# A two-layer attention, linear-attention and MLP backbone on one core: the MLP phases' arithmetic leaves GpSimd for VectorE

## The chip, the cores and the metric

The kernel runs on one core of a Trainium2 chip. The metric is device time of one execution in microseconds. Three executions of the kernel before took 2741.91, 2745.80 and 2748.45 us; the median is 2745.8 us. Engines are named as in the profile: PE multiplies matrices, DVE is VectorE, ACT is ScalarE, POOL is GpSimd, SP issues the DMAs.

## The reference

512 latent tokens and 256 context tokens of width 1024 pass through two layers. Each layer mixes tokens (windowed attention and a gated linear attention, merged and projected) and then runs a squared-ReLU MLP of width 4096. Cut to what the change touches:

```
def rms_norm(x, g):
    y = x * rsqrt(mean(x * x) + EPS); return y * g
def modulate(h, shift, scale):
    return h * (1.0 + scale) + shift
def squared_relu_mlp(h, w1, w2):
    return square(relu(h @ w1)) @ w2
# per layer, after the token mixing:
x  = x  + gt2  * squared_relu_mlp(modulate(rms_norm(x,  g_norm2), sh2,  sc2),  w_ff1, w_ff2)
xc = xc + gt2c * squared_relu_mlp(modulate(rms_norm(xc, g_norm2), sh2c, sc2c), w_ff1, w_ff2)   # not in the last layer
```

All of it is in float32; the last layer has no context stream in its MLP, so its token width is 512 where the first layer's is 768.

## The kernel before, in words

**Split products.** A float32 operand is split in two: a high part, rounded to the matmul's reduced float32 format by ACT (`act(hi, src, Copy)`), and a low part, source minus high part, by a `tensor_tensor` subtraction on DVE or POOL. `split` does it for activations and `unit` for a 512 KB weight tile (names `raw`, `whi`, `wlo`). A product is three matmuls: high by high, high by low, low by high.

**The MLP** (`mlp`) runs over 8 chunks of 512 hidden columns. Chunk 0 multiplies `w_ff1` directly (`ff1`, `relu2`). After its products `seven_tokens` builds the token factors of a 2 by 2 block scheme with seven products instead of eight: for each of 4 row blocks four sums `b` (high plus low part of the normed input H), then differences that are split into `T` and back into H. Chunks 1 to 7 use `seven_weights` (weight factors `s1` to `s4`, each split) and `seven` (seven products into three PSUM banks, with `cw`, `cz` and `c` holding partial results, and `ended` squaring the ReLU and splitting it into `hid`). Every chunk ends with the second product: four panels of `w_ff2`, each added into x by a DVE instruction on line 1065.

**The junction.** The last thing before chunk 0's second product is the norm of tokens 256 to 511 (`late`), whose result H the first product, the token factors and so all later chunks need. Below, "junction" means this stretch: 1060 to 1105 us in the first layer, 2378 to 2421 us in the second. "Chunk loop" means chunks 1 to 7: about 1130 to 1590 us and 2440 to 2710 us.

**Norm.** `norm` makes 8 row blocks of H. Blocks 1, 3 and 5 go through `split` with the low part on POOL, the others through line 337 on DVE.

**What sets the order.** Instructions of an engine run in order. That order is chosen when the program is built, by a scheduler that steps a timing model and picks among the instructions that are ready; tile pools decide when a buffer is free: 3 `raw`, 4 `whi`, 4 `wlo`, 8 `c` or `b` tiles, 5 `mm` banks in the MLP. The same helper lines stand for all users: line 97 is every ACT copy or activation, line 100 every subtraction, line 106 every addition, line 103 every multiplication; so the tile names tell them apart.

Of the kernel before, what the change touches and what calls it, by code (L numbers as in the profile page):

```python
# [10 lines left out]
F32 = mybir.dt.float32  # L11
# [19 lines left out]
CH = 512  # L31
# [28 lines left out]
class Net:  # L60
# [259 lines left out]
    def norm(self, x, t0, n, which, H, rs=None):  # L320

        nc = self.nc
        tt = slice(t0, t0 + n)
        c = int(t0 >= SEQ)
        A, sh = self.A[which], self.mod[:, 0 if which == 1 else 3]
        rs = self.scales(x, t0, n) if rs is None else rs
        for k in range(KD):
            xr = self.t2([128, n], "xr")
            b = sh[:, k, c:c + 1]
            nc.vector.scalar_tensor_tensor(out=xr, in0=x[:, k, tt], scalar=A[:, k, c:c + 1], in1=rs, op0=ALU.mult, op1=ALU.mult)  # L330
            if k % 2 and k < 7:
                nc.vector.tensor_scalar_add(xr, xr, b)
                self.split(H, xr, (slice(None), k, tt), nc.gpsimd)
            else:
                hi = H.hi[:, k, tt]
                self.act(hi, xr, ACTF.Identity, bias=b)
                nc.vector.scalar_tensor_tensor(out=H.lo[:, k, tt], in0=xr, scalar=b, in1=hi.bitcast(F32),
                                               op0=ALU.add, op1=ALU.subtract)
# [585 lines left out]
    def seven_weights(self, w, c0):  # L924

        nc = self.nc
        raws = []
        for r in (0, 512):
            raw = self.wp.tile([128, 4, 2, 128], F32, name="raw", tag="raw", bufs=3)
            nc.sync.dma_start(out=raw, in_=w[r:r + 512, c0:c0 + 256].rearrange("(k p) (f c) -> p k f c", p=128, f=2))  # L930
            raws.append(raw)
        a11, a21 = raws[0][:, :, 0], raws[0][:, :, 1]
        a12, a22 = raws[1][:, :, 0], raws[1][:, :, 1]
        s1, s2, s3, s4 = [self.t2([128, 4, 128], n) for n in ("s1", "s2", "s3", "s4")]
        self.add(s1, a21, a22)
        self.sub(s2, s1, a11)
        self.sub(s3, a11, a21, nc.gpsimd)
        self.sub(s4, a12, s2)
        out = {}
        for group in ((("a11", a11), ("s2", s2)), (("s1", s1), ("a12", a12)), (("s3", s3), ("s4", s4)), (("a22", a22),)):  # L940
            hi = self.wp.tile([128, 2, 4, 128], F32R, name="whi", tag="whi")
            lo = self.wp.tile([128, 2, 4, 128], F32R, name="wlo", tag="wlo")
            for i, (name, src) in enumerate(group):
                self.act(hi[:, i], src, ACTF.Copy)
                self.sub(lo[:, i], src, hi[:, i].bitcast(F32))
                out[name] = [Pair(hi[:, i, k], lo[:, i, k]) for k in range(4)]
        return out

    def seven_tokens(self, pool, H, n):

        nc = self.nc
        wide = self.wide([128, 2, 2, 4, n], F32R, "T12")
        t4 = pool.tile([128, 2, 4, n], F32R, name="T4", bufs=1)
        T = {"t1": Pair(wide[:, 0, 0], wide[:, 0, 1]), "t2": Pair(wide[:, 1, 0], wide[:, 1, 1]),
             "t4": Pair(t4[:, 0], t4[:, 1])}
        at = {"b11": (0, 0), "b21": (4, 0), "b22": (4, n), "t3": (0, n)}

        def temp(name):
            return pool.tile([128, n], F32, name=name, tag="c", bufs=8)

        for k in range(4):
            b = {}
            for name, (r, t0) in (("b12", (0, n)), ("b11", (0, 0)), ("b22", (4, n)), ("b21", (4, 0))):
                b[name] = temp(name)
                self.add(b[name], H.hi[:, r + k, t0:t0 + n].bitcast(F32), H.lo[:, r + k, t0:t0 + n].bitcast(F32), nc.gpsimd)
            self.sub(b["b11"], b["b12"], b["b11"])
            self.split(T["t1"], b["b11"], (slice(None), k))
            self.sub(b["b11"], b["b22"], b["b11"])
            self.split(T["t2"], b["b11"], (slice(None), k))
            self.sub(b["b21"], b["b21"], b["b11"])  # L970
            self.split(T["t4"], b["b21"], (slice(None), k))
            self.sub(b["b22"], b["b22"], b["b12"])
            self.split(H, b["b22"], (slice(None), k, slice(n, 2 * n)))
        out = {name: [Pair(t.hi[:, k], t.lo[:, k]) for k in range(4)] for name, t in T.items()}
        for name, (r, t0) in at.items():
            out[name] = [Pair(H.hi[:, r + k, t0:t0 + n], H.lo[:, r + k, t0:t0 + n]) for k in range(4)]
        return out

    def seven(self, pool, W, X, n, hid):

        nc = self.nc

        def part(ps, a, b, start):
            self.product(ps, n, list(zip(W[a], X[b])), start)

        def temp(name):
            return pool.tile([128, n], F32, name=name, tag="c", bufs=8)

        def ended(c, f, t0):
            h = hid[f]  # L990
            nc.vector.scalar_tensor_tensor(out=c, in0=c, scalar=0.0, in1=c, op0=ALU.max, op1=ALU.mult)
            self.split(h, c, (slice(None), slice(t0, t0 + n)), nc.gpsimd)

        a, b, c = [self.bank("mm") for _ in range(3)]
        s, w, z, c11, c12, c21, c22 = [temp(name) for name in ("cs", "cw", "cz", "c11", "c12", "c21", "c22")]
        part(a, "a11", "b11", True)
        self.act(s, a[:, :n], ACTF.Copy)
        part(b, "s2", "t2", True)
        self.add(w, b[:, :n], s)
        part(c, "s1", "t1", True)  # L1000
        self.add(z, c[:, :n], s)
        part(a, "a12", "b21", False)
        self.act(c11, a[:, :n], ACTF.Relu)
        ended(c11, 0, 0)
        part(b, "s3", "t3", False)
        self.add(c22, b[:, :n], z)
        ended(c22, 1, n)
        part(c, "s4", "b22", False)
        self.add(c12, c[:, :n], w)
        ended(c12, 0, n)  # L1010
        part(b, "a22", "t4", False)
        self.add(c21, b[:, :n], s)
        ended(c21, 1, 0)

    def mlp(self, l, x, H, groups, late, before_last, done):


        nc, io, tc = self.nc, self.io, self.tc
# [4 lines left out]
        with tc.tile_pool(name="ml", bufs=1, reuse_waits="tile") as pool:  # L1023
            for ch in range(nch):
# [10 lines left out]
                if ch == 0:  # L1035
                    us = [self.panel(io["w_ff1"][l], p * 256) for p in range(2)]
# [15 lines left out]
                    before_last()  # L1052
                for part in (groups if ch == nch - 1 else [whole]):
                    for p in range(4):
                        us = self.panel(io["w_ff2"][l], p * 256, rows=(ch * CH, (ch + 1) * CH), lo_eng=nc.gpsimd)
                        for f in range(2):
                            j = p * 2 + f
                            for t0, n in part:
                                c, xx = int(t0 >= SEQ), x[:, j, t0:t0 + n]
                                ps = self.mm()  # L1060
                                self.product(ps, n, [(Pair(us[0].hi[:, k, f * 128:(f + 1) * 128],
                                                           us[0].lo[:, k, f * 128:(f + 1) * 128]),
                                                      Pair(h.hi[:, t0:t0 + n], h.lo[:, t0:t0 + n]))
                                                     for k, h in enumerate(hid)])
                                nc.vector.scalar_tensor_tensor(out=xx, in0=ps[:, :n],  # L1065
                                                               scalar=self.mod2[:, 5, j, c:c + 1], in1=xx,
                                                               op0=ALU.mult, op1=ALU.add)
                            self.tick(0.7)
                    if ch == nch - 1:
                        done(part)  # L1070
# [136 lines left out]
```

## Time and profile before

| | |
|---|---|
| median of three executions | 2745.8 us |
| the profiled execution's own time | 2742.91 us |
| its span in the profile | 2741.1 us |
| granted PE clock, mean | 0.972 |
| PE busy | 2579.2 us (94%) |
| DVE busy | 1634.7 us (60%) |
| ACT busy | 1151.7 us (42%) |
| POOL busy | 780.1 us (28%) |

An engine's busy time does not tell whether it holds up another; that is read from the idle time ahead of an instruction and from what ended it (in brackets in a timeline). A duration of a DVE or POOL instruction runs from its start to its end, so time in which it is held is inside it. The granted clock is a share of PE's full 2.4 GHz; 0.5 is 1.2 GHz.

### The profile page before, as it was taken

To read this page: it belongs to the slowest core of one execution; us is meant where nothing else is said; L and a number is where in the kernel's file an instruction comes from. 1 tells how busy PE (TensorE), PEld (TensorE's weight loads), DVE (VectorE), ACT (ScalarE), POOL (GpSimd) and SP (SyncE) were. 2 spreads that over 40 slices of the span, in tenths; PEclk is the share of its full clock that TensorE was granted. 3 is DMA by queue.
4 is the path that set the end of the run, shared out by engine and by line. 5 is a ranking of instruction groups with operands and counts; after the bars stand their busy time and mean duration, and the time that the engine had idled before them with its cause. 6 is when DMAs were issued, how large, how long until landed. Compare 5 with 4: busy or idle time off the path is not lost. (4 is left out here: it accounts for less than half of the span.)

```text
span 2741.1 us, 43359 instructions
## 1 busy us (share of the span) xinstructions
PE 2579.2 (94%) x17227; PEld 2267.8 (83%) x17227; DVE 1634.7 (60%) x3127; ACT 1151.7 (42%) x2526; POOL 780.1 (28%) x574
## 2 busy tenths in 40 slices
PE   6899999999999898999999988999999998889999
PEld 3888887878878787888888988888888887879898
DVE  4566777534454468644455565787654446677765
ACT  3556554435252334322222245655445334434343
POOL 1413221211120214232223354233122112253444
PEclk7999999999999999999999999999999999999999
DMA  7212123233343433243333241222222225322333
GB/s 252 68 36 72 45 49 100 89 101 93 100 139 90 159 109 93 85 131 107 124 116 123 77 149 47 66 63 68 88 77 85 62 85 177 108 92 90 103 106 111
DMA packets 223838, 269.82 MB, mean 98 GB/s; under 512 B 18480, under 2 KB 185684, under 8 KB 223508
## 3 DMA queue, kind: packets, MB, share of 16 engines
q1 hardware_dynamic: 223636, 267.05, 32.0%
q8 instruction: 135, 2.21, 0.3%
q14 instruction: 67, 0.55, 0.1%
HBM read 244.21 MB, written 22.81 MB: 97 GB/s over the span
## 5 line engine op out<-in xcount | busy, mean ns | idle before, releaser
L97 ACT ACTIVATE whi<-raw 128x1024 fp32r<-128x1024 f32 (+1 forms) x350 | 333.0, 953 | 585.7 <-DMA raw<-in_w_ff 167.2
L920 PE MATMUL mm<-hid,whi 128*128 128x512 f32 (+1 forms) x1664 | 427.3, 347 | 21.0 <-ACT hid L97 10.1
L100 POOL TENSOR_TENSOR wlo<-raw,whi 128x1024 fp32r<-128x1024 f32 x126 | 306.1, 2434 | 321.4 <-ACT whi L97 295.4
L920 PEld LDWEIGHTS mm<-hid,whi 128*128 128x128 f32 x1664 | 290.5, 192 | 72.5 <-issue 11.9
L100 DVE TENSOR_TENSOR wlo<-raw,whi 128x1024 fp32r<-128x1024 f32 (+1 forms) x224 | 238.2, 1064 | 141.2 <-ACT whi L97 137.6
L920 PE MATMUL mm<-hid,wlo 128*128 128x256 f32 (+1 forms) x832 | 281.5, 343 | 0.0
L173 PE MATMUL mm<-H,whi 128*128 128x512 f32 (+1 forms) x760 | 263.0, 347 | 4.8 <-POOL H L100 4.3
L172 PE MATMUL mm<-H,whi 128*128 128x512 f32 (+1 forms) x760 | 264.0, 350 | 2.9 <-ACT H L97 2.1
L174 PE MATMUL mm<-H,wlo 128*128 128x512 f32 (+1 forms) x760 | 261.7, 345 | 0.0
L1065 DVE SCALAR_TENSOR_TENSOR x<-mm,mod,x 128x512 f32<-128x512 f32 (+1 forms) x208 | 126.6, 622 | 125.4 <-PE mm L920 125.1
L920 PE MATMUL mm<-H,whi 128*128 128x384 f32 (+1 forms) x896 | 197.6, 311 | 0.0
L100 POOL TENSOR_TENSOR hid<-c,hid 128x384 fp32r<-128x384 f32 (+1 forms) x112 | 112.4, 1013 | 248.3 <-ACT hid L97 244.0
L920 PEld LDWEIGHTS mm<-hid,wlo 128*128 128x128 f32 x832 | 158.8, 191 | 18.1
L173 PEld LDWEIGHTS mm<-H,whi 128*128 128x128 f32 x760 | 146.6, 193 | 21.0 <-POOL H L100 4.8
L172 PEld LDWEIGHTS mm<-H,whi 128*128 128x128 f32 x760 | 146.4, 194 | 19.9 <-ACT H L97 2.8
L174 PEld LDWEIGHTS mm<-H,wlo 128*128 128x128 f32 x760 | 146.5, 193 | 16.3 <-issue 0.2
L920 PEld LDWEIGHTS mm<-H,whi 128*128 128x128 f32 x896 | 149.8, 190 | 9.4 <-issue 4.9
L920 PE MATMUL mm<-T,whi 128*128 128x384 f32 (+1 forms) x672 | 145.2, 309 | 0.0
L920 PE MATMUL mm<-H,wlo 128*128 128x384 f32 (+1 forms) x448 | 137.5, 309 | 1.1 <-DVE wlo L100 1.1
L97 ACT ACTIVATE p<-p,nm 128x512 f32<-128x512 f32 (+1 forms) x128 | 98.1, 768 | 71.6 <-DVE nm L456 71.6
L453 DVE CUSTOM_DVE_ANT_0 p<-S,mask 128x512 f32<-128x512 f32 (+1 forms) x128 | 96.3, 752 | 46.3 <-PE S L451 44.5
L100 POOL TENSOR_TENSOR mz<-mz,az 128x256 f32<-128x256 f32 (+1 forms) x32 | 36.4, 1137 | 301.3 <-ACT az L97 189.5
(276 smaller groups left out, 6768.3 us busy)
## 6 DMA issues: line engine op xcount, KB each, us to landing
raw<-in_w_ff SPq DMA_DIRECT2D x136, 512.0 KB
raw<-in_w_mod SPq DMA_DIRECT2D x96, 512.0 KB
raw<-in_w_in SPq DMA_DIRECT2D x88, 512.0 KB
raw<-in_w_branch_attn SPq DMA_DIRECT2D x64, 256.0 KB
raw<-in_w_out SPq DMA_DIRECT2D x32, 512.0 KB
raw<-in_w_in SPq DMA_DIRECT2D x32, 256.0 KB
ya<-yd SPq DMA_DIRECT2D x32, 256.0 KB
raw<-in_w_branch_gla SPq DMA_DIRECT2D x16, 512.0 KB
```

The costliest lines, as they stand in the source:

```text
L97: return self.nc.scalar.activation(out=out, in_=in_, func=func, **kw)
L100: (eng or self.nc.vector).tensor_tensor(out=out, in0=a, in1=b, op=ALU.subtract)
L172: nc.tensor.matmul(ps[:, :n], lhsT=wh, rhs=xh, start=(i == 0), stop=False)
L173: nc.tensor.matmul(ps[:, :n], lhsT=wh, rhs=xl, start=False, stop=False)
L174: nc.tensor.matmul(ps[:, :n], lhsT=wl, rhs=xh, start=False, stop=(i == len(ks) - 1))
L453: nc.vector.tensor_tensor_reduce(out=p[:, :nk], in0=S[:, s0:s0 + nk], in1=mask, scale=1.0, scalar=-3e38, op0=ALU.add, op1=ALU.max, accum_o ...
L920: self.nc.tensor.matmul(ps[:, :n], lhsT=a, rhs=b, start=start and i == j == 0, stop=i == last and j == 2, skip_group_check=not start)
L1065: nc.vector.scalar_tensor_tensor(out=xx, in0=ps[:, :n], scalar=self.mod2[:, 5, j, c:c + 1], in1=xx, op0=ALU.mult, op1=ALU.add)
```

## The change

Five places lose their POOL argument, so that the same instruction is issued on DVE: the low parts of norm's blocks 1, 3 and 5 (norm runs in the token mixing's start too), the weight factor `s3`, the sums `b` of `seven_tokens`, the low parts of `hid` in `ended`, and the low parts of the `w_ff2` panels. In the MLP phases POOL has no arithmetic left; in the token mixing it keeps its own.

```
--- before.py
+++ after.py
@@ -330,7 +330,7 @@
             nc.vector.scalar_tensor_tensor(out=xr, in0=x[:, k, tt], scalar=A[:, k, c:c + 1], in1=rs, op0=ALU.mult, op1=ALU.mult)
             if k % 2 and k < 7:
                 nc.vector.tensor_scalar_add(xr, xr, b)
-                self.split(H, xr, (slice(None), k, tt), nc.gpsimd)
+                self.split(H, xr, (slice(None), k, tt))
             else:
                 hi = H.hi[:, k, tt]
                 self.act(hi, xr, ACTF.Identity, bias=b)
@@ -934,7 +934,7 @@
         s1, s2, s3, s4 = [self.t2([128, 4, 128], n) for n in ("s1", "s2", "s3", "s4")]
         self.add(s1, a21, a22)
         self.sub(s2, s1, a11)
-        self.sub(s3, a11, a21, nc.gpsimd)
+        self.sub(s3, a11, a21)
         self.sub(s4, a12, s2)
         out = {}
         for group in ((("a11", a11), ("s2", s2)), (("s1", s1), ("a12", a12)), (("s3", s3), ("s4", s4)), (("a22", a22),)):
@@ -962,7 +962,7 @@
             b = {}
             for name, (r, t0) in (("b12", (0, n)), ("b11", (0, 0)), ("b22", (4, n)), ("b21", (4, 0))):
                 b[name] = temp(name)
-                self.add(b[name], H.hi[:, r + k, t0:t0 + n].bitcast(F32), H.lo[:, r + k, t0:t0 + n].bitcast(F32), nc.gpsimd)
+                self.add(b[name], H.hi[:, r + k, t0:t0 + n].bitcast(F32), H.lo[:, r + k, t0:t0 + n].bitcast(F32))
             self.sub(b["b11"], b["b12"], b["b11"])
             self.split(T["t1"], b["b11"], (slice(None), k))
             self.sub(b["b11"], b["b22"], b["b11"])
@@ -989,7 +989,7 @@
         def ended(c, f, t0):
             h = hid[f]
             nc.vector.scalar_tensor_tensor(out=c, in0=c, scalar=0.0, in1=c, op0=ALU.max, op1=ALU.mult)
-            self.split(h, c, (slice(None), slice(t0, t0 + n)), nc.gpsimd)
+            self.split(h, c, (slice(None), slice(t0, t0 + n)))
 
         a, b, c = [self.bank("mm") for _ in range(3)]
         s, w, z, c11, c12, c21, c22 = [temp(name) for name in ("cs", "cw", "cz", "c11", "c12", "c21", "c22")]
@@ -1052,7 +1052,7 @@
                     before_last()
                 for part in (groups if ch == nch - 1 else [whole]):
                     for p in range(4):
-                        us = self.panel(io["w_ff2"][l], p * 256, rows=(ch * CH, (ch + 1) * CH), lo_eng=nc.gpsimd)
+                        us = self.panel(io["w_ff2"][l], p * 256, rows=(ch * CH, (ch + 1) * CH))
                         for f in range(2):
                             j = p * 2 + f
                             for t0, n in part:
```

The scheduler orders the program anew. Three places on DVE follow, as the difference of the two orders; a leading minus is before, a plus is now. First, DVE in the first layer's junction (`hid` is the low part of the activations of chunk 0, `x` the addition of a second product, `b_11423<-H` one of the 16 sums of `seven_tokens`):

```order
-L100 TENSOR_TENSOR hid<-r,hid 128x256 x2
+L100 TENSOR_TENSOR hid<-r,hid 128x256
 L100 TENSOR_TENSOR T_11381<-b_11385,T_11381 128x384
-L100 TENSOR_TENSOR b_11405<-b_11403,b_11405 128x384
+L1065 SCALAR_TENSOR_TENSOR x<-mm,mod,x 128x256
+L112 COPY lcol<-pt 128x74
+L100 TENSOR_TENSOR hid<-r,hid 128x256 x3
+L100 TENSOR_TENSOR b_11409<-b_11409,b_11405 128x384
+L100 TENSOR_TENSOR b_11407<-b_11407,b_11403 128x384
+L100 TENSOR_TENSOR T_11381<-b_11405,T_11381 128x384
+L106 TENSOR_TENSOR b_11423<-H 128x384
```

The last three low parts of `hid` are now ahead of the second half of the sums: 8 of the 16 sums stand behind them.

Second, DVE in the second layer's junction (`wlo` is the low part of a `w_ff2` panel, `r` the squaring of chunk 0's ReLU):

```order
 L100 TENSOR_TENSOR b_24180<-b_24180,b_24176 128x256
 L100 TENSOR_TENSOR b_24178<-b_24178,b_24174 128x256
+L100 TENSOR_TENSOR hid<-r,hid 128x256
 L100 TENSOR_TENSOR T_24152<-b_24176,T_24152 128x256
+L100 TENSOR_TENSOR b_24196<-b_24194,b_24196 128x256
+L106 TENSOR_TENSOR b_24198<-H 128x256
+L100 TENSOR_TENSOR wlo<-raw,whi 128x1024
+L103 TENSOR_TENSOR r<-r 128x256 x2
+L106 TENSOR_TENSOR b_24200<-H 128x256
+L103 TENSOR_TENSOR r<-r 128x256
+L106 TENSOR_TENSOR b_24214<-H 128x256
```

Here 14 of the 16 sums, and four low parts of panels, stand ahead of the last `hid`.

Third, DVE in the second layer's chunk loop (`cw`, `cz` and `c` read PSUM; the 128x1024 `wlo` is a panel's low part):

```order
 L106 TENSOR_TENSOR cw<-mm,cs 128x256
+L100 TENSOR_TENSOR wlo<-raw,whi 128x1024
 L106 TENSOR_TENSOR cz<-mm,cs 128x256
+L100 TENSOR_TENSOR hid<-c_27006,hid 128x256
+L100 TENSOR_TENSOR wlo<-raw,whi 128x1024
 L991 SCALAR_TENSOR_TENSOR c_27151<-c_27151 128x256
 L106 TENSOR_TENSOR c_27154<-mm,cz 128x256
 L991 SCALAR_TENSOR_TENSOR c_27154<-c_27154 128x256
+L100 TENSOR_TENSOR hid<-c_27151,hid 128x256
```

The panels' low parts and those of `hid`, which were on POOL's own queue, now stand between the instructions that empty PSUM.

## Rows read from the trace of the kernel before

**Rows 1.** The page's head: span, and busy time of each engine.
```profile
span 2741.1 us, 43359 instructions
...
PE 2579.2 (94%) x17227; PEld 2267.8 (83%) x17227; DVE 1634.7 (60%) x3127; ACT 1151.7 (42%) x2526; POOL 780.1 (28%) x574
```
**Rows 2.** Five stretches: length, busy PE, PEld, DVE, ACT, POOL, then granted clock, DMA.
```profile
1130.00:1590.00 460.00, 457.59 (x2755) 398.54 (x2755) 234.42 (x374) 124.08 (x205) 146.43 (x96) 1.00 0.36 114
2440.00:2710.00 270.00, 270.00 (x1738) 247.18 (x1737) 192.03 (x299) 108.33 (x199) 126.08 (x93) 1.00 0.33 102
1060.00:1105.00 45.00, 33.25 (x212) 29.67 (x211) 41.89 (x57) 18.30 (x41) 31.47 (x22) 0.85 0.20 60
2378.00:2421.00 43.00, 28.09 (x133) 23.91 (x134) 38.12 (x59) 17.22 (x39) 31.43 (x24) 0.68 0.15 48
1680.00:1990.00 310.00, 292.15 (x2308) 256.26 (x2307) 217.96 (x554) 167.64 (x413) 85.10 (x55) 0.98 0.25 67
```
**Rows 3.** Timeline of PE, first layer's junction: start, length, idle before with releaser.
```profile
1068.94 0.58 PE L173 MATMUL mm<-H,whi 128*128 128x256 f32 x1 [2.74 <-POOL H L100]
...
1085.49 1.23 PE L920 MATMUL mm<-hid,whi 128*128 128x512 f32 x3 [4.01 <-ACT hid L97]
...
1091.84 0.50 PE L920 MATMUL mm<-hid,whi 128*128 128x256 f32 x2 [2.13 <-ACT r L97]
...
1095.59 0.79 PE L920 MATMUL mm<-hid,whi 128*128 128x512 f32 x1 [2.87 <-DVE hid L100]
```
**Rows 4.** Timeline of PE, second layer's junction.
```profile
2388.71 0.58 PE L173 MATMUL mm<-H,whi 128*128 128x256 f32 x1 [1.53 <-POOL H L100]
...
2406.40 2.08 PE L920 MATMUL mm<-hid,whi 128*128 128x512 f32 x4 [6.07 <-ACT hid L97]
...
2412.49 0.80 PE L920 MATMUL mm<-hid,whi 128*128 128x512 f32 x1 [4.02 <-DVE hid L100]
```
**Rows 5.** Timeline of POOL, then of DVE, at one moment of the first junction.
```profile
1075.63 2.58 POOL L100 TENSOR_TENSOR wlo<-raw,whi 128x1024 fp32r<-128x1024 f32 x1
...
1075.87 2.62 DVE L103 TENSOR_TENSOR r<-r 128x256 f32<-128x256 f32 x1
```
**Rows 6.** DVE groups by shape, 1061 to 1105: count, busy, mean ns, idle before.
```profile
L103 DVE TENSOR_TENSOR r<-r 128x256 f32<-128x256 f32 x8 | 10.1, 1266 | 0.0
L100 DVE TENSOR_TENSOR b<-b,b 128x384 f32<-128x384 f32 x12 | 9.2, 777 | 1.9 <-POOL b L106 1.8
L100 DVE TENSOR_TENSOR T<-b,T 128x384 fp32r<-128x384 f32 x8 | 8.2, 1020 | 0.0
L100 DVE TENSOR_TENSOR hid<-r,hid 128x256 fp32r<-128x256 f32 x8 | 6.1, 785 | 0.0
```
**Rows 7.** DVE groups by shape, 2381 to 2421.
```profile
L100 DVE TENSOR_TENSOR b<-b,b 128x256 f32<-128x256 f32 x16 | 16.5, 1048 | 2.4 <-POOL b L106 1.3 <-DVE b L100 0.5
L100 DVE TENSOR_TENSOR T<-b,T 128x256 fp32r<-128x256 f32 x11 | 9.2, 855 | 0.0
```
**Rows 8.** POOL groups by shape, 1061 to 1105.
```profile
L106 POOL TENSOR_TENSOR b<-H 128x384 f32<-128x384 f32 x16 | 21.0, 1328 | 18.8 <-DVE H L337 12.9 <-DVE T L100 3.7 <-DVE b L100 1.7
L100 POOL TENSOR_TENSOR wlo<-raw,whi 128x1024 fp32r<-128x1024 f32 x3 | 7.9, 2644 | 0.0
```
**Rows 9.** Timeline of DVE: instructions that nothing held, in two stretches.
```profile
1615.61 1.21 DVE L100 TENSOR_TENSOR wlo<-raw,whi 128x1024 fp32r<-128x1024 f32 x1
...
2414.71 0.74 DVE L100 TENSOR_TENSOR hid<-r,hid 128x256 fp32r<-128x256 f32 x2
```
**Rows 10.** Timeline of DVE in the second layer's chunk loop.
```profile
2620.61 2.70 DVE L991 SCALAR_TENSOR_TENSOR c<-c 128x256 f32<-128x256 f32 x1 [2.30 <-ACT c L97]
2623.23 0.41 DVE L106 TENSOR_TENSOR c<-mm,cz 128x256 f32<-128x256 f32 x1
```
**Rows 11.** POOL groups by shape in the second layer's chunk loop, 2440 to 2710.
```profile
L100 POOL TENSOR_TENSOR wlo<-raw,whi 128x1024 fp32r<-128x1024 f32 x27 | 65.2, 2415 | 12.0 <-ACT whi L97 11.6
L100 POOL TENSOR_TENSOR hid<-c,hid 128x256 fp32r<-128x256 f32 x54 | 46.5, 872 | 106.8 <-ACT hid L97 106.8
```

More of the change, by code (lines that the diff above doesn't have):

```diff
@@ L332, in norm @@
                 nc.vector.tensor_scalar_add(xr, xr, b)
-                self.split(H, xr, (slice(None), k, tt), nc.gpsimd)
+                self.split(H, xr, (slice(None), k, tt))
             else:
@@ L936, in seven_weights @@
         self.sub(s2, s1, a11)
-        self.sub(s3, a11, a21, nc.gpsimd)
+        self.sub(s3, a11, a21)
         self.sub(s4, a12, s2)
@@ L964, in seven_tokens @@
                 b[name] = temp(name)
-                self.add(b[name], H.hi[:, r + k, t0:t0 + n].bitcast(F32), H.lo[:, r + k, t0:t0 + n].bitcast(F32), nc.gpsimd)
+                self.add(b[name], H.hi[:, r + k, t0:t0 + n].bitcast(F32), H.lo[:, r + k, t0:t0 + n].bitcast(F32))
             self.sub(b["b11"], b["b12"], b["b11"])
@@ L991, in ended @@
             nc.vector.scalar_tensor_tensor(out=c, in0=c, scalar=0.0, in1=c, op0=ALU.max, op1=ALU.mult)
-            self.split(h, c, (slice(None), slice(t0, t0 + n)), nc.gpsimd)
+            self.split(h, c, (slice(None), slice(t0, t0 + n)))
         a, b, c = [self.bank("mm") for _ in range(3)]
@@ L1054, in mlp @@
                     for p in range(4):
-                        us = self.panel(io["w_ff2"][l], p * 256, rows=(ch * CH, (ch + 1) * CH), lo_eng=nc.gpsimd)
+                        us = self.panel(io["w_ff2"][l], p * 256, rows=(ch * CH, (ch + 1) * CH))
                         for f in range(2):
```

## The prediction

> **What bounds the kernel now.** I read the page's head first: PE is busy for 2579.2 of 2741.1 us, so whatever is gained or lost must show as idle time, or half-clock time, of PE; DVE's 60% and POOL's 28% alone decide nothing [rows 1]. Then the busy time by stretch. In the two chunk loops, 460 and 270 us, PE has no idle time worth naming (2.4 us and none) at a granted clock of 1.00: a faster or slower DVE there changes the time only from the point at which PE starts to wait. In the two junctions PE works 33.25 of 45 and 28.09 of 43 us, the clock falls to 0.85 and 0.68, and DVE is nearly full (41.89 and 38.12 us) while POOL has 31 us of work in each [rows 2]. So the junctions are where this change can pay.
>
> Next the timeline of PE there: what ended each stall. In the first junction 2.74 us ended with a low part of H from POOL, then 4.01, 2.13 and 2.87 us with `hid` or `r` of chunk 0, 11.75 us in all [rows 3]. In the second it is 1.53 us on POOL's H, then 6.07 and 4.02 us on `hid`, 11.62 us in all [rows 4]. `hid` comes from ACT and DVE, not from POOL, so the last step is to ask why they are late. A DVE multiplication of 256 columns starts 0.24 us after a POOL low part that runs 2.58 us, takes 2.62 us and ends with it [rows 5]; the same kind of instruction beside nothing takes 0.41 us (two in a row 0.74, so a further one costs 0.33) [rows 9]. DVE is being held for whole POOL instructions. ACT's copies for T and `hid` wait in line for DVE's results, so PE's `hid` waits carry POOL's time.
>
> By the Trainium skill (SBUF — State Buffer, Who interferes with whom) a DVE instruction with two SBUF inputs and a GpSimd instruction that reads SBUF exclude each other, the first to start holding the shared port to its end. It adds one thing to these rows: a DVE instruction that reads PSUM and only one SBUF operand would be untouched, so by that rule the relief reaches the factors and `hid`, but not the additions into x. The sum below uses no figure of it.
>
> **The change part by part.**
>
> *The junctions, what goes.* I take the excess of each DVE group over its free duration. Free is 0.41 us for 256 columns and 1.21 for 1024 [rows 9]; for 384 columns I interpolate to 0.545, an estimate from these two. First junction: r 8 x (1.266 - 0.41) = 6.8, b 12 x (0.777 - 0.545) = 2.8, T 8 x (1.020 - 0.545) = 3.8, hid 8 x (0.785 - 0.41) = 3.0, together 16.4 us, and 1.8 us in which DVE stood waiting for POOL's b: 18.2 us [rows 6]. Second: b 16 x (1.048 - 0.41) = 10.2, T 11 x (0.855 - 0.41) = 4.9, and 1.3 us of waiting: 16.4 us [rows 7].
>
> *The junctions, what comes.* POOL did 16 sums b and the low parts of three panels here [rows 8], and three low parts of H. On DVE each costs one step in a row, 0.08 us under its duration: 0.465 us for 384 columns, 0.33 for 256, 1.13 for 1024. Only what stands ahead of the last `hid` counts for PE. In the first layer the order of the changed kernel has 8 sums, 3 H and 3 panels ahead: 3.7 + 1.0 + 3.4 = 8.1 us. In the second it has 14 sums, 3 H and 4 panels: 4.6 + 1.0 + 4.5 = 10.1, and one `s3` chain member of 512 columns, some 0.6 us by interpolation: 10.7 us.
>
> *The junctions, net.* DVE's chain to the last `hid` shortens by 18.2 - 8.1 = 10.1 and 16.4 - 10.7 = 5.7 us. Both are under the stalls of 11.75 and 11.62 us that PE has to give, so I count them in full: 15.8, rounded to 16 us. Bounds: at most all stalls, 23.4 us, and if the clock then also stayed up, the second junction's 0.68 over 43 us leaves some room beyond its stalls; I allow 10 us for both, so 33 us. At least: nothing, if ACT or the relu of late PE products ends the wait instead; and below nothing, if the panels' low parts, 7 x 1.13 = 8 us, hit exactly the `hid` that PE waits for. I take 16 because two ways to the same PE stall, the excess and the list of stalls, agree.
>
> *The chunk loops: 0 us.* In the second layer's loop POOL did 27 panel low parts and 54 of `hid` [rows 11]; with `s3` for 12 more, DVE gets 27 x 1.13 + 54 x 0.33 + 12 x 0.6 = 55.5 us and loses the holding beside POOL. Even with nothing lost it would have 192 + 55.5 = 248 of 270 us [rows 2], so it still fits; in the first layer's loop 234 of 460 us leaves far more room. What hides it is PE's own queue, and how much delay that cover takes can be read: a squaring on DVE there took 2.70 us, held as in the junctions, with an addition out of PSUM queued behind it [rows 10], and PE did not wait [rows 2]. In the new order at most one panel low part of 1.21 us stands ahead of such an instruction at a time, less than the delay that is borne already. Bounds: no gain, since PE has no idle time there; a loss of one 1.21 us wait in each of 14 chunks, 17 us. I take nothing, the row being on that side.
>
> *Norms elsewhere and the second layer's attention: 0 us.* Three low parts of 0.33 us in each norm replace POOL ones; between the two layers the order on PE changes up to the end of the second attention. That stretch has 310 - 292.15 = 17.9 us of PE idle time [rows 2], whose waits are mostly between DVE and PE; I allow a quarter of it, 4.5 us, both ways.
>
> *Sum.* Against the profiled execution, 2741.1 us of span in 2742.9 us: 2742.9 - 16 = 2726.9. It lies 2.9 us under the median of the three runs, so for a median I forecast 2745.8 - 16 = 2730 us.
>
> **The rivals.**
>
> *Hidden anyway.* The chain shortens but PE waits for something else: chunk 0's `r` needs ACT after PE's own last ff1 products, and PE restarts at half clock whatever DVE does. For it: one of the seven stalls ended with ACT's r, not with DVE [rows 3], and the clock is already low when ff1 begins again. Against it: six of the seven ended with a product of DVE, POOL or of ACT behind them [rows 3, 4]. Time: 2745.8 +- 4.5, say 2745 us.
>
> *All of it.* Both junctions lose their stalls and the clock stays up: 2745.8 - 33 = 2713 us. For it: the clock falls only where PE idles. Against it: DVE stays nearly full in the junctions, so some wait remains.
>
> *Panels ahead of evictions (slower).* In each chunk four low parts of 1.21 us wait in DVE's queue for ACT's high part, which waits until PE gives up a weight buffer; behind them stand the additions that empty the three banks PE needs next. It costs from the point at which that wait passes the slack of two products. Two such waits per chunk, 28 x 1.21 = 34 us, less the 16 us: 2764 us. For it: the new order puts them there. Against it: the 2.70 us squaring that PE bore [rows 10].
>
> *DVE is the bound and gets more.* If POOL were not what stretches DVE (both merely wait for H), the added work is paid in full: 8.1 + 10.7 us more, 2765 us. For it: DVE is 93% and 89% busy in the junctions [rows 2]. Against it: durations of one shape that differ sixfold [rows 5, 9]. The Trainium skill (Perfetto Trace Analysis, Optimizing Scalar/DVE Operations) points that way: with a saturated DVE, handing work to GpSimd may make sense; it adds that the shared port might undo this, which is how I read the rows here.
>
> **How the numbers follow.** Forecast 0.64, with its own range of 2722 to 2738 us; all of it 0.08; hidden anyway 0.18; panels ahead of evictions 0.06; DVE as the bound 0.04. A measurement of this kernel tells about 0.2%, 5.5 us, from no change: below 2740.3 counts as faster, above 2751.3 as slower. The first two cases and a small part of the third are faster: 0.74. The rest of the third is the same: 0.16. The last two are slower: 0.10. The range for 8 in 10 reaches from the edge of the "all of it" case to the middle of the hidden case: 2713 to 2747 us.
>
> **What would show it.** Right: in the junctions DVE's r, b, T and `hid` at 0.41 and about 0.55 us with no long ones; no PE stall ended by POOL; the stalls on `hid` down to 1 to 2 us in the first layer and about 5 in the second; the chunk loops still full for PE, DVE there at some 80% in the second layer. Wrong: PE idle in the chunk loops ahead of a product, released by `cw`, `cz` or `c`; or the junctions as long as now with DVE's durations short, which would be the hidden case.

## The result, and the profile after

The changed kernel takes 2713.8 us (median of five, 2710.1 to 2719.2) against 2744.6 us for the kernel before (median of five, 2741.6 to 2748.5): ratio 0.989, interval 0.9872 to 0.9908. It is 30.8 us faster; 16 were forecast. The time lies 0.8 us above the lower end of the range, 16.2 us under the predicted 2730. The profiled execution took 2711.4 us, 31.5 less than the one of before.

The head of the page after, against [rows 1]:
```profile
span 2709.6 us, 43214 instructions
...
PE 2564.4 (95%) x17227; PEld 2258.0 (83%) x17227; DVE 1685.8 (62%) x3404; ACT 1153.5 (43%) x2526; POOL 382.0 (14%) x297
```
POOL gave up 398 us of work, yet DVE's busy time rose by only 51 us: the taken-over instructions came, and the time in which DVE had been held went. The stretches, first and second junction ahead of their loops (columns as in [rows 2]; each stretch starts where that layer's last norm does, 2 us earlier in the first layer and 17 us in the second):
```profile
1058.00:1103.00 45.00, 44.52 (x304) 38.13 (x303) 43.26 (x94) 21.20 (x47) 0.00 (x0) 1.00 0.32 98
1110.00:1570.00 460.00, 455.84 (x2761) 399.43 (x2760) 277.52 (x474) 125.33 (x204) 0.00 (x0) 1.00 0.36 113
2361.00:2404.00 43.00, 36.96 (x187) 31.07 (x188) 40.73 (x98) 20.16 (x44) 0.00 (x0) 0.88 0.20 62
2415.00:2680.00 265.00, 265.00 (x1696) 242.06 (x1695) 212.80 (x384) 105.99 (x194) 0.00 (x0) 1.00 0.33 102
```
The first junction is now a full stretch for PE (44.52 of 45 us, before 33.25), at a granted clock of 1.00 instead of 0.85. In the second PE works 36.96 of 43 us instead of 28.09, at 0.88 instead of 0.68. In the second loop PE is as full as before, with DVE at 80%; in the first it is idle for 4.16 of 460 us, before for 2.41. One of its waits there (0.62 us at 1268.78) ended with `cw`, which the prediction gave as a sign of being wrong: it occurred once.

PE's stalls in the two junctions behind the norms' matmuls, from its timeline (start, length, idle before with releaser), against [rows 3, 4]:
```profile
1065.25 0.39 PE L173 MATMUL mm<-H,whi 128*128 128x256 f32 x1 [0.48 <-DVE H L100]
...
2364.79 1.22 PE L172 MATMUL mm<-H,whi 128*128 128x256 f32 x4 [2.08 <-ACT H L97]
...
2381.18 0.50 PE L920 MATMUL mm<-hid,whi 128*128 128x512 f32 x1 [1.45 <-ACT r L97]
2382.58 0.80 PE L920 MATMUL mm<-hid,whi 128*128 128x512 f32 x1 [0.90 <-DVE hid L100]
2388.68 0.50 PE L920 MATMUL mm<-hid,whi 128*128 128x512 f32 x1 [0.99 <-DVE hid L100]
```
The first layer keeps 0.48 of 11.75 us. In the second, the waits of [rows 4] shrink from 11.62 to 3.34 us, with none left on POOL. The wait of 2.08 us on ACT's H, and one of 0.48 us that is not shown, are the same in both kernels. DVE's groups in the first junction, 1058 to 1113 us (count, busy, mean ns, idle before), against [rows 6]:
```profile
L100 DVE TENSOR_TENSOR b<-b,b 128x384 f32<-128x384 f32 x16 | 8.5, 563 | 0.0
L106 DVE TENSOR_TENSOR b<-H 128x384 f32<-128x384 f32 x16 | 8.5, 564 | 0.0
L100 DVE TENSOR_TENSOR T<-b,T 128x384 fp32r<-128x384 f32 x12 | 6.7, 563 | 0.0
...
L100 DVE TENSOR_TENSOR hid<-r,hid 128x256 fp32r<-128x256 f32 x8 | 3.2, 428 | 0.0
L103 DVE TENSOR_TENSOR r<-r 128x256 f32<-128x256 f32 x8 | 3.1, 426 | 0.0
```
T fell from 1020 to 563 ns, r from 1266 to 426. The sums b, which took POOL 1328 ns each [rows 8], take DVE 564. No shape is long any more.

The next place to look is DVE's way from the norm's first instruction (line 330) to the end of the last `hid`, which PE needs for the second product. Before, in the first and in the second layer (the last `hid` of the second stands in [rows 9]):
```profile
1061.17 2.07 DVE L330 SCALAR_TENSOR_TENSOR xr<-x,A,rs 128x256 f32<-128x256 f32 x5 [4.33 <-ACT rs L97]
...
1101.98 0.75 DVE L100 TENSOR_TENSOR hid<-r,hid 128x256 fp32r<-128x256 f32 x2
...
2381.46 2.07 DVE L330 SCALAR_TENSOR_TENSOR xr<-x,A,rs 128x256 f32<-128x256 f32 x5 [2.46 <-ACT rs L97]
```
and after:
```profile
1059.74 2.07 DVE L330 SCALAR_TENSOR_TENSOR xr<-x,A,rs 128x256 f32<-128x256 f32 x5 [4.32 <-ACT rs L97]
...
1083.34 1.10 DVE L100 TENSOR_TENSOR hid<-r,hid 128x256 fp32r<-128x256 f32 x3
...
2363.71 2.07 DVE L330 SCALAR_TENSOR_TENSOR xr<-x,A,rs 128x256 f32<-128x256 f32 x5 [2.27 <-ACT rs L97]
...
2388.19 1.11 DVE L100 TENSOR_TENSOR hid<-r,hid 128x256 fp32r<-128x256 f32 x3
```
In the first layer it is 24.7 us now instead of 41.6, 16.9 less; in the second 25.6 instead of 34.0, 8.4 less.

The same marks on PE's timeline, taken in every kernel, cut the span into stretches; below, each is given as its length less that of the kernel before, in us, from one profiled execution each. A junction runs here from the start of the last norm's last matmul on line 314 to that of the first product with T, which comes a little later than the window's end; "loop 1" ends with the first layer's last product with `hid`; "attention" is from there to the end of the second layer's attention; "tail" is from the last product with T to the end of the matmuls. The first 1017 us, where of the change only the norm's low parts stand (in e11 and e12 more), differ by -4.0 to +4.4 between executions; a difference there is left out.

| kernel | junction 1 | loop 1 | attention 2 | junction 2 | loop 2 | tail |
|---|---|---|---|---|---|---|
| after | -15.0 | -2.6 | +3.2 | -11.6 | +0.5 | -2.7 |
| e1 only sums | -8.5 | -1.2 | +0.4 | -5.5 | 0.0 | 0.0 |
| e2 only panels | -6.3 | +0.8 | +4.2 | -3.4 | +0.5 | -2.7 |
| e3 only norm | -0.7 | -2.4 | -0.4 | +0.4 | 0.0 | 0.0 |
| e4 only loop | +0.2 | +1.3 | -1.0 | -0.6 | +1.9 | +0.3 |
| e5 idle sums | -6.6 | -3.3 | +1.5 | -11.6 | +0.5 | -2.7 |
| e6 without norm | -10.7 | -2.5 | +4.1 | -11.7 | +0.5 | -2.7 |
| e7 without panels | -10.8 | +0.2 | -1.5 | -6.6 | +1.7 | +0.3 |
| e8 without sums | -7.5 | -2.5 | -0.2 | -7.2 | +0.5 | -2.7 |
| e9 idle sums, late | -4.9 | -1.8 | +2.9 | -9.4 | +0.5 | -2.7 |
| e10 without loop | -15.1 | +1.9 | +0.3 | -10.2 | +0.5 | -2.7 |
| e11 kd, merge too | -15.0 | -2.1 | -4.5 | -12.4 | +0.5 | -2.7 |
| e12 nothing on POOL | -15.0 | -3.3 | -13.6 | -12.7 | +0.5 | -2.7 |

Junction 1 and the tail repeat to 0.02 us between kernels that leave them alone (after, e11, e12). Loop 1 does not: e3, which changes nothing in chunks 1 to 7, has -2.4 there, so a difference of that size is not told from none.

So 15.05 + 11.61 = 26.66 of the 31.5 us lie in the junctions.

### The profile page after: what moved, and what is told of

Same layout as the page of the kernel before. It is cut to its first block, busy times and chain, and to the rows that moved or that the text cites. A ratio compares the mean times of both kernels' runs of the same rounds, so it can differ in the third digit from the quotient of the medians.

```text
span 2709.6 us, 43214 instructions
## 1 busy us (share of the span) xinstructions
PE 2564.4 (95%) x17227; PEld 2258.0 (83%) x17227; DVE 1685.8 (62%) x3404; ACT 1153.5 (43%) x2526; POOL 382.0 (14%) x297
## 5 line engine op out<-in xcount | busy, mean ns | idle before, releaser
L100 DVE TENSOR_TENSOR wlo<-raw,whi 128x1024 fp32r<-128x1024 f32 (+1 forms) x296 | 322.7, 1091 | 182.3 <-ACT whi L97 179.0
L920 PE MATMUL mm<-hid,wlo 128*128 128x512 f32 (+1 forms) x832 | 282.6, 342 | 0.0
L100 POOL TENSOR_TENSOR wlo<-raw,whi 128x1024 fp32r<-128x1024 f32 x54 | 129.4, 2405 | 204.6 <-ACT whi L97 166.5
L920 PEld LDWEIGHTS mm<-T,whi 128*128 128x128 f32 x672 | 112.5, 190 | 2.0 <-issue 0.4
L184 PE MATMUL mm<-whi,H 128*128 128x256 f32 x384 | 110.9, 289 | 0.0
```

The source lines that it names most:

```text
L100: (eng or self.nc.vector).tensor_tensor(out=out, in0=a, in1=b, op=ALU.subtract)
L184: nc.tensor.matmul(ps, lhsT=xh, rhs=u.hi[:, k], start=(i == 0), stop=False)
L920: self.nc.tensor.matmul(ps[:, :n], lhsT=a, rhs=b, start=start and i == j == 0, stop=i == last and j == 2, skip_group_check=not start)
```

## The experiments

Three theories ran through them. H: a GpSimd instruction holds DVE's instructions on two SBUF operands, and PE waits for that. L: PE waits for GpSimd's own results, which come late. O: only the new order of instructions counts. Each kernel is set against runs of the kernel before that were taken beside it. The interval of "after" is some 5 us to either side, so a difference of less than that against "after" is read from the table, not from the times.

**One part alone (e1 to e4).** Each is one line of the change on the kernel before (e4: two).
```diff
# e1
-                self.add(b[name], H.hi[...].bitcast(F32), H.lo[...].bitcast(F32), nc.gpsimd)
+                self.add(b[name], H.hi[...].bitcast(F32), H.lo[...].bitcast(F32))
# e2
-   us = self.panel(io["w_ff2"][l], p * 256, rows=(ch * CH, (ch + 1) * CH), lo_eng=nc.gpsimd)
+   us = self.panel(io["w_ff2"][l], p * 256, rows=(ch * CH, (ch + 1) * CH))
# e3
-                self.split(H, xr, (slice(None), k, tt), nc.gpsimd)
+                self.split(H, xr, (slice(None), k, tt))
# e4
-        self.sub(s3, a11, a21, nc.gpsimd)
+        self.sub(s3, a11, a21)
-            self.split(h, c, (slice(None), slice(t0, t0 + n)), nc.gpsimd)
+            self.split(h, c, (slice(None), slice(t0, t0 + n)))
```


> Only the 16 sums b of each seven_tokens go to VectorE. Theory H (holding: a GpSimd instruction stops VectorE's two-input instructions for its length, and the junctions' stalls of TensorE are that time; once they are short the clock does not fall either): the sums are 21.0 and 15.9 us of GpSimd in the junctions, more than half of its work there, so about 10 to 15 us off the kernel before, near 2732. Theory L (late results: TensorE waits because GpSimd's own results come late, about twice VectorE's durations): the same 10 to 15 us, since VectorE waits for b directly. Theory O (order: the gain comes from the new order alone): any value.

> Only the low parts of the w_ff2 panels go to VectorE. Theory H: 3 and 4 holds of 2.6 us in the junctions turn into 1.13 us each, so 4 to 8 us off, near 2738; chunk loops unchanged. Theory L: no stall of TensorE ended with a panel's low part on GpSimd, so 0 to 1 us off, near 2744. Theory O: any value.

> Only norm's three low parts go to VectorE. Theory H: they are 2.8 and 2.5 us of 31 us of GpSimd work in each junction, so 2 to 4 us off, near 2741. Theory L: the stalls of 2.74 and 1.53 us that end with H from GpSimd go, and with them the first fall of the clock: 5 to 8 us off, near 2738. Theory O: any value.

> Only hid's low parts and s3, all of them in chunks 1 to 7, go to VectorE. All theories: TensorE has no idle time in the chunk loops, so nothing there; at the end of the second layer's loop the 1.48 us stall on GpSimd's hid shortens: 0 to 2 us off, near 2743.

Measured against 2744.5 us: e1 2729.7 (ratio 0.9944, 0.9931 to 0.9958), e2 2736.5 (0.9967, 0.9954 to 0.9980), e3 2742.0 (0.9992, 0.9981 to 1.0002), e4 2750.1 (1.0019, 1.0010 to 1.0029). The sums' 14.8 us fit H and L alike. The panels' 8.0 us fit H and not L, which had 0 to 1. The norm's 2.5 us are not told from none, and are less than L's 5 to 8. In medians the four changes sum to -14.8 - 8.0 - 2.5 + 5.7 = -19.6 us, while the whole change gives -30.8. The table shows a part of that difference: in the first junction the four add up (-15.2 against -15.0), in the second they make -9.1 of -11.6. What stands in for the missing part there is in e1's PE, second junction:
```profile
2395.68 0.50 PE L920 MATMUL mm<-hid,whi 128*128 128x512 f32 x1 [1.16 <-DVE hid L100]
2403.92 0.80 PE L920 MATMUL mm<-hid,wlo 128*128 128x512 f32 x1 [6.13 <-POOL wlo L100]
```
With the sums gone from POOL, `hid` is early, and PE waits 6.13 us for a panel's low part, which is still on POOL. This is L's kind of wait; in the kernel before, none ended so. So L is not wrong, it is second in line.

e4 is a miss: every theory had it at no loss. Its second loop, 2440 to 2710 us, DVE groups and one instruction of its timeline:
```profile
L991 DVE SCALAR_TENSOR_TENSOR c<-c 128x256 f32<-128x256 f32 x53 | 46.8, 893 | 2.7 <-ACT c L97 2.5
L100 DVE TENSOR_TENSOR hid<-c,hid 128x256 fp32r<-128x256 f32 x52 | 45.6, 877 | 8.7 <-ACT hid L97 6.6
...
2460.93 2.48 DVE L100 TENSOR_TENSOR hid<-c,hid 128x256 fp32r<-128x256 f32 x1 [0.49 <-ACT hid L97]
```
and POOL, whose only work there is the panels' low parts:
```profile
L100 POOL TENSOR_TENSOR wlo<-raw,whi 128x1024 fp32r<-128x1024 f32 x26 | 63.4, 2448 | 226.6 <-DVE cw L106 205.0 <-ACT whi L97 21.6
```
The squarings and the low parts of `hid` are now both on DVE and both held, 893 and 877 ns. The loop is 1.9 us longer, and 1.7 in e7, the only other kernel with this split (`hid` on DVE, panels on POOL). The way is H's own. In six of the chunks one low part of `hid` is held like the one shown: it starts 0.20 us after a panel's low part on POOL and takes 2.48 us. PE's product that needs it starts as it ends, and the steps between matmuls are some 0.28 us longer there than elsewhere, too short to be listed as a wait: 6 x 0.28 = 1.7 us. In e7 it happens five times. At the end of that loop the wait of 1.48 us on POOL's `hid` did not shorten, as was expected, but became 0.70 us on DVE's `c` and 1.23 on ACT's `hid`. The rest of e4's 5.7 us stays open.

**The change without one part (e6, e7, e8, e10).** Each is the kernel after with the lines above as they were before: e6 those of e3, e7 of e2, e8 of e1, e10 of e4. For e7:
```diff
-   us = self.panel(io["w_ff2"][l], p * 256, rows=(ch * CH, (ch + 1) * CH))
+   us = self.panel(io["w_ff2"][l], p * 256, rows=(ch * CH, (ch + 1) * CH), lo_eng=nc.gpsimd)
```


> The changed kernel with norm's three low parts back on GpSimd. Theory H: GpSimd then has 3 short instructions per junction, 1 to 3 us slower than the changed kernel. Theory L: TensorE's stall on H of 2.7 and 1.5 us comes back, and with it the fall of the clock: 4 to 8 us slower.

> The changed kernel with the panels' low parts back on GpSimd. Theory H: 3 and 4 holds of about 2.6 us per junction less 1.13 us each on VectorE: 3 to 8 us slower than the changed kernel; chunk loops as they are. Theory L: 0 to 2 us slower, the panel's low part itself being late at most at the first panel.

> The changed kernel with the sums b back on GpSimd. Theories H and L alike: 8 to 14 us slower than the changed kernel, since both the holding and the waits for b come back. If the parts of the change add up, this loss equals the gain of the sums alone.

> The changed kernel with hid's low parts and s3 of chunks 1 to 7 back on GpSimd. Alone this pair had made the kernel before 5 us slower. If the pair costs VectorE something whenever it is there, the kernel is 2 to 5 us faster than the changed one; if it cost only because GpSimd's panel low parts held the moved instructions, the kernel is as the changed one or up to 3 us slower, since GpSimd now holds VectorE in the chunk loops, which TensorE bears.

Measured: e6 2719.7 (0.9910, 0.9896 to 0.9924), e7 2729.6 (0.9942, 0.9929 to 0.9954), e8 2727.1 (0.9934, 0.9921 to 0.9946) against 2745.7; e10 2718.5 (0.9901, 0.9888 to 0.9915) against 2745.2. Against after that is +5.8, +15.8, +13.3 and +4.7 us.

- e6: 5.8 us are in L's range and above H's. The norm's three low parts, worth 0.7 us of the first junction alone (e3), are worth 4.3 once the rest is done (-10.7 against -15.0). PE waits 0.72 and 0.96 us for POOL's H there, as L has it, and 1.75 us for a DMA.
- e7: 15.8 us are above both ranges; the panels were put too low. The junctions hold 4.2 + 5.0 us, the loops 2.8 + 1.1 and the tail 2.9, while the second layer's attention is 4.8 shorter there. No wait of PE in its junctions ends with POOL, so L does not show.
- e8: 13.3 us are in the range that H and L shared, and near the 14.8 us that the sums give alone.
- e10: 4.7 us are outside both of its ranges, but within the interval of after. It keeps the first junction whole and loses 1.4 us in the second. It is 4.5 us longer in the first loop, but PE is idle there for 2.5 us, in after for 4.2. So it is not shown that moving the loop's own low parts pays once the panels are off POOL; when they are not, it costs (e4).

**Idle work on POOL (e5, e9).** The kernel after, with 16 sums per junction on POOL that nothing reads. They take away H's gain and nothing else. Nothing reads what POOL makes, what it reads is not written again in `seven_tokens`, and no wait of PE, ACT or DVE in these junctions ends with POOL.
```diff
         idle = pool.tile([128, n], F32, name="idle", bufs=1)
                 self.add(b[name], H.hi[...].bitcast(F32), H.lo[...].bitcast(F32))
# e5: beside the sums of tokens that are ready early
+                for _ in range(0 if t0 else 2):
+                    self.add(idle, H.hi[...].bitcast(F32), H.lo[...].bitcast(F32), nc.gpsimd)
# e9: beside the late tokens' sums of row blocks 4 to 7
+                for _ in range(4 if name == "b22" else 0):
+                    self.add(idle, H.hi[...].bitcast(F32), H.lo[...].bitcast(F32), nc.gpsimd)
```


> The changed kernel, and besides 16 sums of H in each seven_tokens on GpSimd into a tile that nobody reads (each of 8 sums twice): GpSimd's load in the junctions without anything that waits for it. The order on the other engines is the changed kernel's. Theory H: VectorE's instructions in the junctions stretch again beside them, by up to 20 us in each; 6 to 15 us slower than the changed kernel, near 2724. Theory L and theory O: nothing waits for it, so as the changed kernel, near 2714.

> The changed kernel and, as in the run before with sums nobody reads, 16 such sums on GpSimd, but all of blocks 4 to 7 of the late tokens, so that in the second layer too they can only start inside the junction (in the earlier run they ran before it there, and that junction did not move). Theory H: both junctions lengthen, by 3 to 9 us each, 6 to 15 us slower than the changed kernel. Theories L and O: no change.

Measured: e5 2722.1 (0.9915, 0.9900 to 0.9930, against 2745.7), e9 2725.6 (0.9928, 0.9915 to 0.9942, against 2745.2): 8.2 and 11.8 us over after. In e5 the first junction is 8.5 us longer than after and the second is not, since there its sums ran from 2340.81 to 2363.06 us, ahead of the junction. In e9 both are longer, by 10.2 and 2.2 us; the second is less than H's 3 to 9. This is POOL in e9 (timeline):
```profile
1064.85 5.87 POOL L106 TENSOR_TENSOR idle<-H 128x384 f32<-128x384 f32 x4 [90.18 <-issue]
1075.56 23.54 POOL L106 TENSOR_TENSOR idle<-H 128x384 f32<-128x384 f32 x12 [4.83 <-DVE H L100]
```
and DVE's groups in the same junction, 1058 to 1113 us:
```profile
L100 DVE TENSOR_TENSOR b<-b,b 128x384 f32<-128x384 f32 x10 | 8.9, 917 | 0.0
L100 DVE TENSOR_TENSOR T<-b,T 128x384 fp32r<-128x384 f32 x8 | 6.0, 755 | 0.0
L100 DVE TENSOR_TENSOR hid<-r,hid 128x256 fp32r<-128x256 f32 x8 | 5.9, 751 | 0.0
...
L103 DVE TENSOR_TENSOR r<-r 128x256 f32<-128x256 f32 x8 | 3.1, 416 | 0.0
L1068 DVE SCALAR_TENSOR_TENSOR x<-mm,mod,x 128x512 f32<-128x512 f32 x4 | 2.9, 750 | 0.0
```
b, T and `hid` are long again (917, 755, 751 ns against 563, 563, 428), PE waits 2.45 us for a `hid` of DVE, and the clock of 1058 to 1103 us is 0.96 instead of 1.00. Nothing that these sums make is used, so not L. Nor is it O: in both junctions of e5 and e9, PE, ACT and DVE run their instructions in the order of after, by name and shape; DVE only gets less far by the junction's end in two of the four. So H is shown.

**Further along the same road (e11, e12).** The kernel after, with two more operations on DVE (e11), and with all of POOL's remaining arithmetic on DVE (e12), so that POOL only fills constants.
```diff
# e11
-            self.sub(kd[1], rb, kd[0].bitcast(F32), nc.gpsimd)
+            self.sub(kd[1], rb, kd[0].bitcast(F32))
-            self.add(y, y, a, self.nc.gpsimd)
+            self.add(y, y, a)
# e12: the same, and so for r, u, rt, w_q's low parts, m, p3, E, G, ...
-        self.mul(u, xn, s, nc.gpsimd if q else None)
+        self.mul(u, xn, s)
```


> The changed kernel, and besides the keys' low parts (kd) and the addition in merge on VectorE, the two other places where TensorE stalls behind GpSimd or behind VectorE's Y beside GpSimd's additions. Theory H: stalls of about 2.4 us on kd per layer shorten and those on Y (3.7, 2.1 and 3.1 us) lose what GpSimd holds: 3 to 8 us faster than the changed kernel. Theory L: kd's stalls only, 2 to 4 us faster. A new order of the attention can move it by 4 us either way.

> The changed kernel with all remaining GpSimd arithmetic of the token mixing on VectorE too (GpSimd keeps its fills). VectorE is busy for 60 to 85% of the token mixing and GpSimd for 15 to 27%: by durations 54 panel low parts of 2.4 us become 1.2 us, the rest about 170 us becomes about 130. Theory H: the holding goes, so VectorE's load rises little and the kernel is 3 to 12 us faster than the changed one; the rival is that VectorE becomes the bound in the attention, 5 to 20 us slower.

Measured against 2745.2 us: e11 2703.5 (0.9850, 0.9836 to 0.9863), e12 2684.8 (0.9781, 0.9768 to 0.9794). e11 is 10.3 us under after, more than either theory had; 7.8 of them are in the second layer's attention. e12 beats both kernels: 60.4 us under before, 29 under after, more than expected. Busy times, from its page:
```profile
PE 2557.9 (95%) x17227; PEld 2252.5 (84%) x17227; DVE 1758.1 (66%) x3686; ACT 1154.4 (43%) x2526; POOL 3.9 (0%) x15
```
776 us of POOL's work have become 123 us more of DVE's busy time. By the table 16.9 of the 29 us lie in the second layer's attention, where after still has 92 us of POOL's work. That stretch in after, then in e12:
```profile
1599.83:1901.61 301.78, 272.21 (x2145) 243.49 (x2144) 207.45 (x537) 170.97 (x418) 92.24 (x56) 0.96 0.26 66
1598.26:1883.19 284.93, 265.67 (x2141) 238.93 (x2140) 218.71 (x588) 170.78 (x414) 0.00 (x0) 0.98 0.28 69
```
PE's idle time falls there from 29.6 to 19.3 us. Another 7.1 us come from the stretch between the attention and the last norm, with the linear attention (-9.0 against -1.9).

## Why the prediction was wrong, and what of it held

*The mechanism held.* The reading of [rows 5], that DVE is held for whole POOL instructions and PE's waits on `hid` carry it, is shown by e5 and e9, which bring the long durations and part of the stalls back with work that nobody reads. The Trainium skill's addition (SBUF — State Buffer, Who interferes with whom), that a DVE instruction with at most one input in SBUF is not touched, agrees with the trace: the additions into x take 747 ns in the second loop after and 743 before, where POOL had 126 us of work; the squarings c, out of SBUF alone, went from 856 to 421. The rows after, of DVE from 2415 to 2680 us:
```profile
L1065 DVE SCALAR_TENSOR_TENSOR x<-mm,mod,x 128x512 f32<-128x512 f32 x48 | 34.4, 747 | 11.3 <-PE mm L920 11.2
L100 DVE TENSOR_TENSOR wlo<-raw,whi 128x1024 fp32r<-128x1024 f32 x27 | 33.0, 1223 | 8.1 <-ACT whi L97 6.4
...
L100 DVE TENSOR_TENSOR hid<-c,hid 128x256 fp32r<-128x256 f32 x54 | 22.5, 420 | 1.6 <-ACT hid L97 0.3
L991 DVE SCALAR_TENSOR_TENSOR c<-c 128x256 f32<-128x256 f32 x54 | 22.2, 421 | 0.8
```
and before, 2440 to 2710 us:
```profile
L991 DVE SCALAR_TENSOR_TENSOR c<-c 128x256 f32<-128x256 f32 x56 | 47.4, 856 | 17.6 <-ACT c L97 16.4
...
L1065 DVE SCALAR_TENSOR_TENSOR x<-mm,mod,x 128x512 f32<-128x512 f32 x48 | 34.7, 743 | 2.4 <-PE mm L920 2.4
```
*The loops at 0* held in the second layer: its +0.5 us are four matmuls that the new order puts ahead of the mark instead of behind it. The rival of panels ahead of evictions fell with it, PE being full there with 27 low parts on DVE. The rivals "hidden anyway" and "DVE is the bound" fell too: durations are short and the junctions shorter. Behind the last one stood the Trainium skill (Perfetto Trace Analysis, Optimizing Scalar/DVE Operations), by which handing work of a saturated DVE to GpSimd may make sense, unless the shared port undoes it. Here DVE was 93% and 89% busy in the junctions, and taking work back from GpSimd made them shorter: the proviso decided.

*The step that failed is the size of the junctions' net,* 15.8 us forecast, 26.66 measured: 15.05 against 10.1 and 11.61 against 5.7. Two things were wrong in it, DVE's chain to the last `hid` and the clock, which had no price in the sum. The two junctions of the table, before and after (columns as in [rows 2]):
```profile
1059.79:1132.79 73.00, 61.25 (x378) 53.32 (x376) 61.74 (x92) 26.10 (x56) 35.59 (x24) 0.91 0.20 61
2379.84:2436.85 57.01, 42.83 (x206) 36.36 (x205) 50.95 (x77) 20.77 (x45) 33.10 (x25) 0.77 0.15 47
...
1058.37:1116.31 57.94, 57.46 (x385) 49.32 (x383) 54.92 (x116) 25.93 (x57) 0.00 (x0) 1.00 0.27 83
2362.08:2407.48 45.40, 39.51 (x206) 33.39 (x205) 43.77 (x101) 20.79 (x45) 0.00 (x0) 0.89 0.19 58
```
- *The chain was counted too short.* DVE's way to the last `hid` shrank by 16.9 and 8.4 us, not by 10.1 and 5.7. What came was counted right: in the first junction 8 sums, 3 low parts of H and 3 panels, as forecast. What went was not. With half of the sums behind the last `hid`, the differences and low parts made from them went behind it too, which the forecast left ahead: of b, T and H, 18 instructions stood ahead of the last `hid` in the first junction and 9 do now (25 and 18 in the second), some 4 and 2 us by the forecast's own prices. This share is order, not holding. And two groups that were held were left out: the low parts of H on line 337 and those of H made from b. Before, from the norm's first instruction to the last `hid` of the first junction:
```profile
L100 DVE TENSOR_TENSOR b<-b,b 128x384 f32<-128x384 f32 x9 | 7.6, 854 | 1.9 <-POOL b L106 1.8
L100 DVE TENSOR_TENSOR T<-b,T 128x384 fp32r<-128x384 f32 x7 | 7.6, 1087 | 0.0
...
L337 DVE SCALAR_TENSOR_TENSOR H<-xr,mod,H 128x256 fp32r<-128x256 f32 x5 | 3.5, 724 | 0.0
...
L100 DVE TENSOR_TENSOR H<-b,H 128x384 fp32r<-128x384 f32 x2 | 2.7, 1354 | 0.0
```
After, b is there 6 times, T 3 times and H from b not at all, and line 337 takes 482 ns. PE's idle time fell by 11.27 us in the first junction, nearly all that there was, and by 8.29 in the second: 19.6 together, where I had 15.8. That the excess and the list of stalls agreed in the first junction was luck: the chain gave more than PE had to give.
- *The clock was put at nothing.* The other 7.1 us are PE's busy time, 61.25 to 57.46 and 42.83 to 39.51 us, for the same matmuls (eight small ones more in the first). The granted clock rose from 0.91 to 1.00 and from 0.77 to 0.89, between the levels of 1.2 and 2.4 GHz. I had named this, and left it to the upper bound ("if the clock then also stayed up") with a chance of 0.08. The first junction went just that way, the second in part.

*The terms that stood at nothing* hold the other 4.9 us. The tail is -2.7 us in each kernel whose panels are off POOL, and 0.0 to +0.3 in each where they are not. Before, POOL did a panel's low part ahead of the `hid` that PE needed:
```profile
2712.29 2.38 POOL L100 TENSOR_TENSOR wlo<-raw,whi 128x1024 fp32r<-128x1024 f32 x1
2714.63 0.72 POOL L100 TENSOR_TENSOR hid<-c,hid 128x256 fp32r<-128x256 f32 x1
```
and PE stood for it:
```profile
2715.40 0.39 PE L920 MATMUL mm<-hid,whi 128*128 128x256 f32 x1 [1.48 <-POOL hid L100]
```
That is 1.48 of the 2.7 us; some 0.5 more are the four matmuls that went to loop 2, and the rest stays open. The stretch lies behind the last of [rows 2], and the forecast gave it no term. The first loop gave 2.6 us, but PE's idle time there rose from 2.4 to 4.2 us and e3 has nearly the same, so it is not shown to come from the change. The stretches that the table leaves out gave 3.3, some of it the spread of the first 1017 us, and the second loop took 0.5. The attention of the second layer took 3.2, inside the 4.5 that were allowed both ways. Why stays open: e2, e6 and e9 have it as well and e5 half of it, e7, e8 and e10 do not, and no one part of the change tells the two groups apart.

## What to carry to other kernels

Where DVE instructions of one shape differ in length by a factor, look for a GpSimd instruction beside them before counting GpSimd as spare capacity: here its work was better done by DVE itself, all of it (e12), although DVE was the busier engine. Count such a change by all the instructions that stand ahead of the one that the waiting engine needs, in the old order and in the new; give the clock its own term in the sum; and look at the end of the program as at any stretch. A wait too short to be listed can still add up when it comes in every chunk (e4). Test parts together: a wait that one part uncovers (e1's 6.13 us) is another part's gain.

## What the runs showed beyond that

- The holding goes both ways. In e9's second junction one idle sum of 256 columns took POOL 22.16 us, the eleven behind it 0.74 to 1.18 each. The `hid` of [rows 9], which the prediction calls beside nothing, ran beside a panel's low part on POOL that took 4.29 us instead of 2.4: there POOL was the one held.
- For these shapes DVE alone is about twice as fast as POOL alone: 1.22 us (second loop after) against 2.38 for a low part of 128x1024, 0.42 against 0.72 for one of 128x256 (the tail of before, shown above).
- Moving work to the busier engine cut the work itself: POOL's 776 us cost DVE 123.
